# The first output tiles in four rounds of four, the input transposed as it arrives, its squares on ScalarE

## The chip, the cores and the metric

One NeuronCore of one Trainium2 chip runs the whole program in one launch. TensorE (PE) multiplies, VectorE (DVE) and ScalarE (ACT) do the elementwise work and may read PSUM, GpSimd (POOL) does elementwise work in SBUF, and SyncE (SP) issues most of the DMA transfers. The metric is the device time of one execution in microseconds; below 0.2% or so a difference can't be told from none.

## What is computed

The trunk of an encoder: 256 tokens of width 2048 in float32, and two layers. Each layer is a token mixer and a gated MLP with a short convolution, each behind an RMSNorm and added to the residual. Only the start matters here, the first norm and the first projection:

```python
def rms_norm(x, g):
    xf = x.astype(jnp.float32)
    y = xf * lax.rsqrt(jnp.mean(xf * xf, axis=-1, keepdims=True) + EPS)
    return (y * g.astype(jnp.float32)).astype(x.dtype)
...
    for i in range(DEPTH):
        a = rms_norm(h, mix_norm[i])
        ...                               # i = 0: neighbourhood attention
        h = h + mixed
        h = h + conv_glu_ffn(rms_norm(h, ffn_norm[i]), ...)
    return rms_norm(h, final_norm)
```

The first mixer projects `a` to q, k and v (2048 to 3 x 2048), attends within a window with a bias per head, and projects back. The root of the mean square is one number per token. So it can be left out of the projection's input and be multiplied on at its output.

## The kernel before

**Products in two parts.** A float32 matrix is split into a rounded part `hi` and the rest `lo`. `hi` comes from a cast on ScalarE (line 118), `lo` from a subtraction on VectorE (line 119). The activations `a` hold both parts side by side, 256 columns each. A tile of 128 outputs takes, for each 128 inputs (one k, 16 in all), one product of `hi` weights with both parts of `a` (line 156, 512 columns) and one of `lo` weights with the high part (line 159, 256 columns), summed in one of four PSUM tiles `mm`.

**Weights.** `prep_to(n)` brings weights up to chunk n: a DMA on SP's queue into one of five `raw` buffers (line 99), then the cast and the subtraction into one of six `hi` and six `lo` buffers. The main loop at the end of the function goes through `items`, one chunk of one phase each, and calls `prep_to` four chunks ahead (`AHEAD`).

**The order of the work.** The text gives each instruction a place, and work that has to come later is put on a list with `after(n, fn)`, which calls `fn` once n items have been run from where it was called (from the set-up: behind item n). A scheduler of the framework then lays out one queue for each engine: among the instructions that are ready by its reckoning, an engine takes the one that comes first in the text. On the chip each queue is run in that order. A tile with a tag takes one of the buffers of that tag in the order of the text.

**The start.** The first phase projects the q and k of heads 0 to 3, eight output tiles. Its first three tiles (`intro=3`) are interleaved: four rounds over k in steps of four, each round with the three tiles, so that work can start before all of x has come. The other five tiles take chunks of eight k. x comes transposed, in eight loads of 256 KB on SP (line 608), two k each. For each, ScalarE multiplies with the norm's weight and rounds (line 187), and VectorE gives the rest (line 188). GpSimd squares x (line 614) and adds up some of the squares (line 616); in `first_stats` VectorE adds the others (line 622), TensorE sums over the partitions with a matrix of ones (`stats`, line 229), and `rsqrt` takes the root over all 256 tokens, the same in every partition; two small products (line 626) turn it into a column for each half of the tokens.

A finished output tile is scaled by this `rstd` in `normed`: ScalarE copies the right half out of PSUM into a `corr` tile (three buffers), VectorE adds the left half, and then multiplies by `rstd`. Until `first_stats` the finished tiles are held in the text.

The residual `h` holds x by token. It is made by transposing x on TensorE with the identity (`to_tokens`, line 603), copied by VectorE or ScalarE (line 604); this stands behind items 12 to 19. The identity comes with the rest of the parameters, at the end of the set-up (line 618).

**Bias.** Each head's bias is loaded on GpSimd's queue into one of two buffers (line 399) and gets the mask added (line 400); `scores` reads it (line 420).

**Warm-up.** Eight products of a matrix of ones (line 80) run on TensorE before anything has come.

Elsewhere the text has a second way to the root, `token_rstd`, for sums of squares by token: a reduction, `rsqrt` on two columns, and one product with a diagonal matrix (line 259) to spread it over all partitions. The later norms use it.

Of the kernel before, what the change touches and what calls it, by code (L numbers as in the profile page):

```python
# [15 lines left out]
F32 = mybir.dt.float32  # L16
F32R = mybir.dt.float32r
AF = mybir.ActivationFunctionType
# [4 lines left out]
P = 128  # L23
D = 2048
S = 256
KT = D // P
# [8 lines left out]
CH = 8  # L35
AHEAD = 4

S_DOWN = (2, 5, 8)
S_OUT = (1, 3, 5)

# [2 lines left out]
C_SC = C_NORM + 5 * KT  # L43
# [3 lines left out]
C_ID = C_MASK + GRID_W  # L47
# [4 lines left out]
def trunk(ctx, tc, xT, par, bias, wqk, wv, wo, wsc, wscout, wup, wdown, out):  # L52
    nc = tc.nc
    cp = ctx.enter_context(tc.tile_pool(name="const", bufs=1))
    wp = ctx.enter_context(tc.tile_pool(name="wts", bufs=1))
    ap_ = ctx.enter_context(tc.tile_pool(name="acts", bufs=1))
    tp = ctx.enter_context(tc.tile_pool(name="tmp", bufs=2))
    pm = ctx.enter_context(tc.tile_pool(name="pm", bufs=4, space=PSUM))
    pa = ctx.enter_context(tc.tile_pool(name="pa", bufs=1, space=PSUM))

    pt = cp.tile([P, C_END], F32, name="pt")
    h = cp.tile([P, 2, D], F32, name="h")
    ones = cp.tile([P, P], F32, name="ones")
    rstd = cp.tile([P, S], F32, name="rstd")
    acc = cp.tile([P, S], F32, name="acc")
    NPAD = 3
    pads = [cp.tile([P, S + 2], F32, name=f"pad{i}") for i in range(NPAD)]
    pad_at = [0]
# [4 lines left out]

    nc.vector.memset(ones, 1.0)
    nc.scalar.dma_start(out=pt[:, :C_SC], in_=par[:, :C_SC])

    nc.scalar.copy(out=tp.tile([P, 1], F32, name="m", tag="m"), in_=ones[:, :1])
    warm = pa.tile([P, P], F32, name="st", tag="st")
    for _ in range(8):
        nc.tensor.matmul(warm, lhsT=ones, rhs=ones, start=True, stop=True)  # L80
    for p_ in pads:
        nc.gpsimd.memset(p_[:, 0:S + 2:S + 1], 0.0)
    ident = pt[:, C_ID:C_ID + P]
    mask = pt[:, C_MASK:C_MASK + GRID_W]

    def norm_g(n, k):
        return pt[:, C_NORM + n * KT + k:C_NORM + n * KT + k + 1]
# [6 lines left out]
    def prep_to(n):  # L94
        while len(prepped) < min(n, len(chunks)):
            src, w, kind = chunks[len(prepped)]
            raw = wp.tile([P, CH * P], F32, name="raw", tag="raw", bufs=5)
            if kind == "rows":
                nc.sync.dma_start(out=raw[:, :w], in_=src)
                prepped.append(parts(raw[:, :w]) + (raw,))  # L100
                continue

            nc.sync.dma_start(out=raw.rearrange("p (f c) -> p f c", f=4), in_=src.rearrange("f p c -> p f c"))
            r = raw.rearrange("p (f k c) -> p f k c", f=4, c=P)
            if kind == "cols":
                prepped.append(parts(r) + (raw,))
            else:
                prepped.append(sums(prepped[-1][2].rearrange("p (f k c) -> p f k c", f=4, c=P), r))
# [66 lines left out]
    def after(n, fn):  # L175
        later.append((at[0] + n, fn))
# [9 lines left out]
    def scaled_split(dst, src, g):  # L186
        nc.scalar.activation(dst[:, :S], src, AF.Copy, scale=g)
        nc.vector.scalar_tensor_tensor(out=dst[:, S:], in0=src, scalar=g, in1=dst[:, :S].bitcast(F32),  # L188
                                       op0=ALU.mult, op1=ALU.subtract)

    def act_tile():
        return ap_.tile([P, 2 * S], F32R, name="act", tag="act", bufs=HALF)

    def a_tile():
        return ap_.tile([P, 2 * S], F32R, name="a", tag="a", bufs=KT)

    def normed(dst, ps):

        corr = tp.tile([P, S], F32, name="corr", tag="corr", bufs=3)
        nc.scalar.copy(out=corr, in_=ps[:, S:])  # L200
        nc.vector.tensor_add(out=corr, in0=ps[:, :S], in1=corr)  # L201
        nc.vector.tensor_mul(out=dst, in0=corr, in1=rstd)  # L202
# [13 lines left out]
    def rsqrt(dst, v, r, t, sums):  # L216

        nc.vector.tensor_scalar(out=v, in0=sums, scalar1=1.0 / D, scalar2=EPS, op0=ALU.mult, op1=ALU.add)
        nc.scalar.activation(r, v, AF.Sqrt)
        nc.vector.reciprocal(out=r, in_=r)  # L220
        nc.vector.tensor_mul(out=t, in0=r, in1=r)
        nc.vector.scalar_tensor_tensor(out=t, in0=t, scalar=-0.5, in1=v, op0=ALU.mult, op1=ALU.mult)
        nc.vector.scalar_tensor_tensor(out=dst, in0=t, scalar=1.5, in1=r, op0=ALU.add, op1=ALU.mult)

    def stats(sums):

        ps = pa.tile([P, S], F32, name="st", tag="st")
        for i, x in enumerate(sums):
            nc.tensor.matmul(ps, lhsT=ones, rhs=x, start=i == 0, stop=i == len(sums) - 1)
        v = tp.tile([P, S], F32, name="v", tag="v", bufs=1)  # L230
        rt = tp.tile([P, 2, S], F32, name="rt", tag="s")
        rsqrt(rstd, v, rt[:, 0, :], rt[:, 1, :], ps)

    def residual(t, q, ps):
        x = h[:, t, q * 4 * P:(q + 1) * 4 * P]
# [14 lines left out]
    def token_rstd(ssq):  # L250

        v = tp.tile([P, 2], F32, name="z", tag="z")
        nc.vector.tensor_reduce(out=v, in_=ssq, axis=AX.X, op=ALU.add)
        rsqrt(rcol, v, tp.tile([P, 2], F32, name="m", tag="m"), tp.tile([P, 2], F32, name="m", tag="m"), v)
        diag = tp.tile([P, S], F32, name="conv", tag="conv", bufs=4)
        for t in range(2):
            nc.vector.tensor_scalar_mul(diag[:, t * P:(t + 1) * P], ident, rcol[:, t:t + 1])
        bc = pa.tile([P, S], F32, name="st", tag="st")
        nc.tensor.matmul(bc, lhsT=ones, rhs=diag, start=True, stop=True)
        return bc  # L260
# [119 lines left out]
    a0 = [None] * KT  # L380
# [5 lines left out]
    rcol = cp.tile([P, 2], F32, name="rcol")  # L386

    def qk_evac(f, ps):
        h, which = divmod(f, 2)
        x = heads[h]  # L390
        t = tp.tile([P, S], F32, name="qk", tag="conv", bufs=4)
        normed(t, ps)
        if which == 0:
            x["qk"] = tp.tile([P, 4 * S], F32R, name="qk", tag="qk")
        x["qk"[which]] = x["qk"][:, which * 2 * S:(which + 1) * 2 * S]
        split(x["qk"[which]], t)
        if which == 0:
            b = tp.tile([P, 6 * GRID_W], F32, name="bias", tag="bias")
            nc.gpsimd.dma_start(out=b, in_=bias[:, h, :])
            nc.gpsimd.tensor_add(out=b.rearrange("p (i c) -> p i c", c=GRID_W),  # L400
                                 in0=b.rearrange("p (i c) -> p i c", c=GRID_W),
                                 in1=mask.unsqueeze(1).broadcast_to([P, 6, GRID_W]))
            x["b"] = b
        else:
            after(2, lambda: scores(h))
# [115 lines left out]
    def up_evac(layer, act, forms):  # L521
        def evac(f, ps):
# [11 lines left out]
            else:  # L534
# [3 lines left out]
                if j % 2 == 0:  # L538
                    glu["even"] = c
                elif j % HALF // 2 in S_DOWN:  # L540
                    forms[j % HALF // 2] = make_forms(glu["even"], c)
# [37 lines left out]
    def mlp(layer, a, evac):  # L579
        for half in range(2):  # L580
# [3 lines left out]
                  intro=0 if half else 3)  # L584
            Tokens([(wdown[layer, half], HALF)], act, evac if half else residual, S_DOWN, forms)

    for g in range(NH // 4):
        Phase(wqk, range(8 * g, 8 * g + 8), KT, a0, qk_evac, intro=0 if g else 3, step=CH // 2)
        Values(g, a0)
    Tokens([(wo, KT)], oT, to_norm(1, a1))  # L590
    mlp(0, a1, to_norm(2, a2))
# [2 lines left out]
    mlp(1, a3, last_evac())  # L594


    sq = []

    def to_tokens(k, x):
        tr = pa.tile([P, 2, S], F32, name="tr", tag="o" if k % 4 else "tr")  # L600
        for t in range(2):
            for i in range(2):
                nc.tensor.transpose(tr[:, t, i * P:(i + 1) * P], x[:, i * S + t * P:i * S + (t + 1) * P], ident)
        (nc.scalar.copy if k % 4 else nc.vector.tensor_copy)(out=h[:, :, k * P:(k + 2) * P], in_=tr)

    for k in range(0, KT, 2):
        x = act_tile().bitcast(F32)
        nc.sync.dma_start(out=x.rearrange("p (k t) -> p k t", k=2), in_=xT[:, k:k + 2, :])
        for i in range(2):
            a0[k + i] = a_tile()  # L610
            scaled_split(a0[k + i], x[:, i * S:(i + 1) * S], norm_g(0, k + i))
        prep_to(1 + k // 2)
        sq.append(act_tile().bitcast(F32))
        nc.gpsimd.tensor_mul(out=sq[-1], in0=x, in1=x)
        if 2 <= k < KT // 2:
            nc.gpsimd.tensor_add(out=sq[0], in0=sq[0], in1=sq[-1])
        after(12 + k // 2, lambda k=k, x=x: to_tokens(k, x))
    nc.sync.dma_start(out=pt[:, C_SC:], in_=par[:, C_SC:])

    def first_stats():  # L620
        for x in sq[5:]:
            nc.vector.tensor_add(out=sq[4], in0=sq[4], in1=x)
        stats([x[:, i:i + S] for x in (sq[0], sq[4]) for i in (0, S)])
        col = pa.tile([P, 2], F32, name="st", tag="st")
        for t in range(2):
            nc.tensor.matmul(col[:, t:t + 1], lhsT=rstd[:, t * P:(t + 1) * P], rhs=ident[:, :1], start=True, stop=True)
        nc.vector.tensor_copy(rcol, col)
        waiting.clear()
        evacuate()

    after(11, first_stats)

    for i, (ph, ft, c, k0, ka, kb) in enumerate(items):
        at[0] = i
# [76 lines left out]
```

## Time and profile before

| | |
|---|---|
| median of 3 runs | 2243.61 us (2243.46 to 2244.1) |
| profiled execution, its own time | 2245.07 us |
| its span | 2243.2 us |
| mean granted TensorE clock | 0.995 |
| HBM, mean | 188 GB/s |

A busy share counts the time in which an engine's instructions run; TensorE's is modelled at the ends of its products. PEld is the loading of weights into TensorE, which overlaps with products. In a row of groups the columns are: line, engine, operation, out<-in, shapes, count | busy us, mean ns of one | idle us before them <- what ended it. In a row of stretches: the stretch and its length, the busy us of PE, PEld, DVE, ACT and POOL with the number of instructions, the granted clock, the share of DMA and its rate. In a row of the chain or the timeline: start, length, what. In a row of waits: who <- for whom: us in total, times, the longest.

### The profile page before, as it was taken

The page shows a single profiled execution, that of the slowest core. Times are in us where ns is not written, and L with a number is a line of the kernel's source. Part 1 is how long each engine was busy: PE and PEld are TensorE (multiplying, and loading weights), DVE is VectorE, ACT ScalarE, POOL GpSimd, SP SyncE. Part 2 cuts the span into 40 slices and gives each one's busy share as a digit, 9 for nine tenths or more (in the row PEclk, how much of TensorE's full clock was granted, in tenths as well). Part 3 has the DMA queues.
Part 4 walks back from the last instruction along what each step waited for, and adds up shares of the span by engine and source line. Part 5 has one row for each costly group of instructions (what it writes and reads, how often), then busy time and mean ns, then how long its engine had stood idle before and what let it go on. Part 6 is the DMA issues. An engine that isn't in the chain of part 4 may idle for free.

```text
span 2243.2 us, 31742 instructions
## 1 busy us (share of the span) xinstructions
PE 2218.2 (99%) x11818; PEld 1910.4 (85%) x11818; DVE 1745.4 (78%) x2546; ACT 1218.7 (54%) x1822; POOL 84.6 (4%) x110
## 2 busy tenths in 40 slices
PE   7999999999999999999999999999999999999997
PEld 6888888888888888888888888888888888888886
DVE  7777665787888778887877777898888778887876
ACT  5555554555554555555554444566555545555553
POOL 3110000000000000000000000000000000000000
PEclk8999999999999999999999999999999999999999
DMA  6556555555556665555665565565555566555563
GB/s 226 184 178 187 180 173 183 185 188 189 188 175 188 218 196 190 188 186 178 186 212 189 183 195 179 170 224 186 189 189 187 172 203 213 189 189 189 163 193 125
DMA packets 209690, 420.97 MB, mean 188 GB/s; under 512 B 13313, under 2 KB 136193, under 8 KB 209537
## 3 DMA queue, kind: packets, MB, share of 16 engines
q1 hardware_dynamic: 207792, 414.72, 58.3%
q0 software_dynamic: 1024, 3.15, 0.5%
q8 instruction: 93, 1.52, 0.3%
q10 hardware_dynamic: 720, 1.09, 0.1%
q14 instruction: 61, 0.49, 0.1%
HBM read 416.81 MB, written 2.10 MB: 187 GB/s over the span
## 4 chain that ended last, share of the span: by engine, by line
PE 98%; DVE 1%; DMA 0%; ACT 0%; issue 0%; DVEq 0%; SPq 0%
PE mm L156 42%; PE mm L159 22%; PE mm L306 8%; PE mm L308 8%; PE mm L307 8%; PE mm L476 1%; PE mm L478 1%; PE mm L477 1%; PE mu L307 1%; PE mu L306 1%; PE mu L308 1%; PE tr L247 1%; PE tr L438 0%; DMA act<-in_xT 0%; DVE a L575 0%; PE sc L413 0%
## 5 line engine op out<-in xcount | busy, mean ns | idle before, releaser
L119 DVE TENSOR_TENSOR lo<-raw,hi 128x1024 fp32r<-128x1024 f32 (+1 forms) x820 | 988.6, 1212 | 382.6 <-ACT hi L118 374.7
L118 ACT CAST hi<-raw 128x1024 fp32r<-128x1024 f32 (+1 forms) x820 | 839.5, 1027 | 797.1 <-issue 428.2
L156 PE MATMUL mm<-a,hi 128*128 128x512 f32 x4096 | 1035.1, 394 | 8.3 <-DVE a L188 4.8
L156 PEld LDWEIGHTS mm<-a,hi 128*128 128x128 f32 x4096 | 737.5, 189 | 144.0 <-DVE a L188 8.5
L159 PEld LDWEIGHTS mm<-a,lo 128*128 128x128 f32 x4096 | 562.5, 191 | 40.7
L159 PE MATMUL mm<-a,lo 128*128 128x256 f32 x4096 | 575.3, 283 | 0.0
L306 PE MATMUL mm<-hi,act 128*128 128x512 f32 x780 | 304.6, 390 | 0.0
L308 PE MATMUL mm<-hi,act 128*128 128x512 f32 x780 | 304.0, 390 | 0.0
L307 PE MATMUL mm<-lo,act 128*128 128x512 f32 x780 | 303.5, 389 | 0.0
L212 DVE SCALAR_TENSOR_TENSOR conv<-pad,pt,conv 128x256 f32<-128x256 f32 x384 | 184.6, 482 | 9.3 <-ACT conv L210 2.9
L308 PEld LDWEIGHTS mm<-hi,act 128*128 128x128 f32 x780 | 146.4, 188 | 31.2
L307 PEld LDWEIGHTS mm<-lo,act 128*128 128x128 f32 x780 | 146.5, 188 | 30.4
L306 PEld LDWEIGHTS mm<-hi,act 128*128 128x128 f32 x780 | 146.4, 188 | 30.3
L210 ACT ACTIVATE conv<-pad,pt 128x256 f32<-128x256 f32 x176 | 105.3, 600 | 17.0 <-DVE pad L202 17.0
L201 DVE TENSOR_TENSOR corr<-mm,corr 128x256 f32<-128x256 f32 x256 | 106.5, 417 | 0.6
L200 ACT COPY corr<-mm 128x256 f32<-128x256 f32 x256 | 92.5, 362 | 0.3 <-PE mm L159 0.3
L202 DVE TENSOR_TENSOR pad<-corr,rstd 128x256 f32<-128x256 f32 x176 | 74.9, 427 | 5.7
L119 DVE TENSOR_TENSOR lo<-t,hi 128x1024 fp32r<-128x1024 f32 x30 | 36.7, 1225 | 24.3 <-ACT hi L118 24.3
L353 POOL TENSOR_TENSOR s<-conv 128x128 f32<-128x128 f32 x12 | 5.6, 465 | 1257.1 <-DVE conv L535 746.4
L118 ACT CAST hi<-t 128x1024 fp32r<-128x1024 f32 x30 | 31.5, 1049 | 36.3 <-PE mm L308 33.4
L476 PE MATMUL mm<-hi,a 128*128 128x512 f32 x128 | 50.7, 396 | 0.0
L477 PE MATMUL mm<-lo,a 128*128 128x512 f32 x128 | 49.9, 390 | 0.0
(140 smaller groups left out, 1302.8 us busy)
## 6 DMA issues: line engine op xcount, KB each, us to landing
raw<-in_wup SPq DMA_DIRECT2D x352, 512.0 KB, 3.9
raw<-in_wdown SPq DMA_DIRECT2D x176, 512.0 KB, 4.4
raw<-in_wsc SPq DMA_DIRECT2D x96, 512.0 KB, 4.1
raw<-in_wqk SPq DMA_DIRECT2D x58, 512.0 KB, 3.8
raw<-in_wv SPq DMA_DIRECT2D x32, 512.0 KB, 3.8
raw<-in_wo SPq DMA_DIRECT2D x32, 512.0 KB, 3.5
raw<-in_wscout SPq DMA_DIRECT2D x32, 512.0 KB, 4.2
raw<-in_wqk SPq DMA_DIRECT2D x12, 256.0 KB, 4.2
```

Of the source, the lines that this page charges most:

```text
L118: nc.scalar.copy(out=hv, in_=r)
L119: nc.vector.tensor_sub(out=lv, in0=r, in1=hv.bitcast(F32))
L156: nc.tensor.matmul(ps, lhsT=hi[:, o:o + P], rhs=self.src[k], start=k == 0, stop=False)
L159: nc.tensor.matmul(ps[:, S:], lhsT=lo[:, o:o + P], rhs=self.src[k][:, :S], start=False, stop=k == self.nk - 1)
L200: nc.scalar.copy(out=corr, in_=ps[:, S:])
L201: nc.vector.tensor_add(out=corr, in0=ps[:, :S], in1=corr)
L202: nc.vector.tensor_mul(out=dst, in0=corr, in1=rstd)
L210: nc.scalar.activation(c, x[:, 1:S + 1], AF.Identity, scale=w[1], bias=b)
L212: nc.vector.scalar_tensor_tensor(out=c, in0=x[:, tap:tap + S], scalar=w[tap], in1=c, op0=ALU.mult, op1=ALU.add)
L306: nc.tensor.matmul(ps, lhsT=xh, rhs=wh, start=start, stop=False)
L307: nc.tensor.matmul(ps, lhsT=xh, rhs=wl, start=False, stop=False)
L308: nc.tensor.matmul(ps, lhsT=xl, rhs=wh, start=False, stop=stop)
```

## The change

`INTRO` and `STEP`, both 4, set the interleaved tiles and the k of a round: the first four output tiles go in four rounds of four k. x is loaded a round ahead by `load_x`, put among the items with `after`; its scaling is as before. `to_tokens` for the pairs of a round is called behind the first two items of that round. Behind the transposes, ScalarE squares each half out of PSUM and sums it up by token (`accum_out`), and VectorE copies all eight tiles to `h`. GpSimd's squares, their sums and `stats` are gone; `first_stats` is now `token_rstd` of those sums, behind item 14. The identity is loaded second on ScalarE's queue; mask and other parameters come on SP behind item 6. Biases are loaded on SP instead of GpSimd's queue. Twelve warm-up products instead of eight.

```diff
+INTRO = 4
+STEP = 4
...
-    acc = cp.tile([P, S], F32, name="acc")
...
     nc.scalar.dma_start(out=pt[:, :C_SC], in_=par[:, :C_SC])
+    nc.scalar.dma_start(out=pt[:, C_ID:], in_=par[:, C_ID:])
...
-    for _ in range(8):
+    for _ in range(12):
         nc.tensor.matmul(warm, lhsT=ones, rhs=ones, start=True, stop=True)
...
-    def stats(sums):
...
-            nc.gpsimd.dma_start(out=b, in_=bias[:, h, :])
+            nc.sync.dma_start(out=b, in_=bias[:, h, :])
...
-        Phase(wqk, range(8 * g, 8 * g + 8), KT, a0, qk_evac, intro=0 if g else 3, step=CH // 2)
+        Phase(wqk, range(8 * g, 8 * g + 8), KT, a0, qk_evac, intro=0 if g else INTRO, step=STEP)
...
+    ssq0 = cp.tile([P, 2, KT // 2], F32, name="ssq0")
+    xs = {}
+
+    def load_x(k):
+        xs[k] = act_tile().bitcast(F32)
+        nc.sync.dma_start(out=xs[k].rearrange("p (k t) -> p k t", k=2), in_=xT[:, k:k + 2, :])
+        for i in range(2):
+            a0[k + i] = a_tile()
+            scaled_split(a0[k + i], xs[k][:, i * S:(i + 1) * S], norm_g(0, k + i))
+
+    def to_tokens(k):
         tr = pa.tile([P, 2, S], F32, name="tr", tag="o" if k % 4 else "tr")
         for t in range(2):
             for i in range(2):
-                nc.tensor.transpose(tr[:, t, i * P:(i + 1) * P], x[:, i * S + t * P:i * S + (t + 1) * P], ident)
-        (nc.scalar.copy if k % 4 else nc.vector.tensor_copy)(out=h[:, :, k * P:(k + 2) * P], in_=tr)
...
+                nc.tensor.transpose(tr[:, t, i * P:(i + 1) * P], xs[k][:, i * S + t * P:i * S + (t + 1) * P], ident)
+        for t in range(2):
+            nc.scalar.activation(tp.tile([P, S], F32, name="s", tag="s"), tr[:, t, :], AF.Square,
+                                 accum_out=ssq0[:, t, k // 2:k // 2 + 1])
+        nc.vector.tensor_copy(out=h[:, :, k * P:(k + 2) * P], in_=tr)
 
     def first_stats():
...
+        nc.vector.tensor_copy(rstd, token_rstd(ssq0))
         waiting.clear()
         evacuate()
 
-    after(11, first_stats)
+    for r in range(KT // STEP):
+        for i in range(STEP // 2):
+            k = r * STEP + 2 * i
+            if r:
+                after((r - 1) * INTRO + i, lambda k=k: load_x(k))
+            else:
+                load_x(k)
+                prep_to(1 + i)
+            after(r * INTRO + i, lambda k=k: to_tokens(k))
+    after(INTRO + 2, lambda: nc.sync.dma_start(out=pt[:, C_SC:C_ID], in_=par[:, C_SC:C_ID]))
+    after((KT // STEP - 1) * INTRO + 2, first_stats)
```

More of the change, by code (lines that the diff above doesn't have):

```diff
@@ L223, in rsqrt @@
         nc.vector.scalar_tensor_tensor(out=dst, in0=t, scalar=1.5, in1=r, op0=ALU.add, op1=ALU.mult)
-    def stats(sums):
[L227 to L232, printed above, removed]
     def residual(t, q, ps):
@@ L594, in trunk @@
     mlp(1, a3, last_evac())
-    sq = []
-    def to_tokens(k, x):
+    ssq0 = cp.tile([P, 2, KT // 2], F32, name="ssq0")
[7 more added lines that the diff above has]
+    def to_tokens(k):
         tr = pa.tile([P, 2, S], F32, name="tr", tag="o" if k % 4 else "tr")
@@ L602, in to_tokens @@
             for i in range(2):
[L603 to L617, printed above, removed]
@@ L618, in trunk @@
-    nc.sync.dma_start(out=pt[:, C_SC:], in_=par[:, C_SC:])
-    def first_stats():
[L621 to L627, printed above, removed]
+                nc.tensor.transpose(tr[:, t, i * P:(i + 1) * P], xs[k][:, i * S + t * P:i * S + (t + 1) * P], ident)
```

## The prediction

> **What bounds the kernel now.** I read the busy shares first, then the slices, then the busy time by stretch.
>
> ```profile
> PE 2218.2 (99%) x11818; PEld 1910.4 (85%) x11818; DVE 1745.4 (78%) x2546; ACT 1218.7 (54%) x1822; POOL 84.6 (4%) x110
> ...
> PE   7999999999999999999999999999999999999997
> ```
>
> TensorE is busy all the time but in the first and the last of 40 slices. The change touches only the first. The waits of TensorE after 60 us are one row:
>
> ```profile
> PE tr L438 <- DVE s L428: 1.4, 1, 1.4
> ```
>
> So all that can be won here lies before 70 us, and the question is how much. The stretches:
>
> ```profile
> core 0: us, PE busy (x) PEld busy (x) DVE busy (x) ACT busy (x) POOL busy (x), PEclk, DMA share, GB/s
> ...
> 5.95:33.90 27.95, 19.17 (x82) 13.64 (x82) 19.35 (x26) 12.36 (x24) 12.39 (x10) 0.82 0.72 247
> 33.90:38.70 4.80, 4.79 (x19) 4.00 (x20) 2.84 (x4) 2.73 (x4) 1.28 (x2) 0.64 0.39 151
> 38.70:64.00 25.30, 25.30 (x147) 22.07 (x146) 23.84 (x39) 17.16 (x27) 2.24 (x2) 1.00 0.71 229
> 64.00:70.00 6.00, 4.63 (x29) 3.96 (x28) 6.00 (x12) 4.62 (x12) 2.79 (x3) 1.00 0.35 94
> ```
>
> From 5.95 us (the first real matmul) to 33.9 it is idle for 8.8 us, and the busy time is stretched by a clock of 0.5. How much work was done there is counted from the TensorE groups of that stretch, priced by rows of the chain at full clock:
>
> ```profile
> L156 PE MATMUL mm<-a,hi 128*128 128x512 f32 x30 | 12.3, 510 | 7.6 <-DVE a L188 4.1 <-ACT hi L118 3.4
> L159 PE MATMUL mm<-a,lo 128*128 128x256 f32 x24 | 4.8, 334 | 0.0
> L603 PE MATMUL tr<-pt,act 128*128 128x128 f32 x24 | 3.5, 276 | 2.0 <-DMA act<-in_xT 1.6 <-DVE h L604 0.3
> L229 PE MATMUL st<-act,ones 128*128 128x256 f32 x4 | 1.2, 378 | 0.0
> ```
> ```profile
> 38.71 1.82 PE mm L156 x8
> ...
> 45.77 0.86 PE st L229 x4
> ...
> 48.58 0.95 PE mm L159 x8
> ...
> 55.82 0.34 PE st L626 x4
> ...
> 70.46 0.44 PE tr L603 x4
> ```
>
> A hi product costs 0.23 us, a lo product 0.12, a transpose 0.11, a pass of the sums 0.215. The 27.95 us hold 30 x 0.23 + 24 x 0.12 + 24 x 0.11 + 4 x 0.215 = 13.3 us of work, so 14.6 are lost. From 33.9 to 38.7 the clock is 0.64, so 0.36 of 4.8, 1.7 us, are lost. From 64 to 70 it is idle for 1.4. **The start loses 17.7 us** beside the 5.95 in which little can run.
>
> Why it loses them is in SP's queue:
>
> ```profile
> 0.74 0.39 SPq L608 DMA_DIRECT2D act<-in_xT  x1
> 1.19 1.37 SPq L99 DMA_DIRECT2D raw<-in_wqk  x3
> 2.60 0.43 SPq L608 DMA_DIRECT2D act<-in_xT  x1
> 3.08 8.69 SPq L99 DMA_DIRECT2D raw<-in_wqk  x5
> 11.81 0.43 SPq L618 DMA_DIRECT2D pt<-in_par  x1
> 12.29 0.42 SPq L608 DMA_DIRECT2D act<-in_xT  x1
> ...
> 27.68 0.43 SPq L608 DMA_DIRECT2D act<-in_xT  x1
> ```
> ```profile
> SPq L99 <- DVE lo L119: 43.2, 19, 7.9
> ```
>
> The third x load goes out at 12.3 us and the sixth at 27.7, behind weight loads that wait for one of five raw buffers, which VectorE's `lo` subtraction frees. And VectorE is itself slowed:
>
> ```profile
> L188 DVE SCALAR_TENSOR_TENSOR a<-act,pt,a 128x256 fp32r<-128x256 f32 x16 | 12.4, 811 | 5.4 <-ACT a L187 5.4
> L614 POOL TENSOR_TENSOR act<-act 128x512 f32<-128x512 f32 x8 | 9.5, 1192 | 17.5 <-DMA act<-in_xT 17.5
> L119 DVE TENSOR_TENSOR lo<-raw,hi 128x512 fp32r<-128x512 f32 x12 | 9.4, 800 | 4.8 <-ACT hi L118 4.2 <-PE mm L159 0.6
> L187 ACT ACTIVATE a<-act,pt 128x256 fp32r<-128x256 f32 x16 | 7.3, 501 | 6.3 <-DMA act<-in_xT 4.5 <-DMA pt<-in_par 1.8
> L118 ACT CAST hi<-raw 128x512 fp32r<-128x512 f32 x12 | 7.2, 613 | 8.0 <-PE mm L156 5.2 <-DMA raw<-in_wqk 2.7
> L604 DVE COPY h<-tr 128x512 f32<-128x512 f32 x4 | 2.7, 684 | 2.4 <-PE tr L603 2.4
> L220 DVE RECIPROCAL rt<-rt 128x256 f32<-128x256 f32 x1 | 1.8, 1752 | 0.1
> L425 ACT ACTIVATE s<-s,m 128x256 f32<-128x256 f32 x4 | 2.0, 502 | 0.5 <-DVE m L423 0.5
> L425 ACT ACTIVATION_READ_ACCUMULATOR s<-s,m 128x1 f32 x4 | 0.7, 186 | 0.0
> ```
> ```profile
> 42.09 0.87 DVE L188 SCALAR_TENSOR_TENSOR a<-act,pt,a 128x256 fp32r<-128x256 f32 x2
> ```
>
> The same L188 takes 0.435 us when GpSimd is quiet and 0.81 on the mean, with GpSimd's squares (L614) around it: 16 x 0.375 = 6 us of VectorE that the squares cost.
>
> **The change, part by part.** *Squares, sums and the reciprocal root.* Out go GpSimd's squares and adds, three adds on VectorE, eight passes of the sums on TensorE (8 x 0.215 = 1.7 us) and the four small ones to the token column (0.34); in comes one 128x256 fp32 product of two passes (0.43). TensorE: **1.6 us less work**. VectorE's root now runs on two columns where one step alone took 1.75 us over 256. It has cover on TensorE: three correction tiles free three of the four PSUM tiles without the root, so three output tiles of 16 hi and 16 lo (5.6 us each) can run meanwhile. I cost it at nothing; without this cover the root's chain would stand open.
>
> *ScalarE and VectorE instead.* By the Exp row a square with its accumulator read is 0.5 to 0.69 us; I take 0.55, since the read overlaps the next. A round has four. ScalarE per round: four hi casts 2.4, four scalings 2.0, squares 2.2: 6.6 us. VectorE per round: four lo 2.8 (0.7 each: the row's 0.8 holds GpSimd's disturbance, and a copy of that size takes 0.68), four L188 1.7, two copies of h 1.4: 5.9 us. TensorE per round: four items of four hi and four lo at 1.4, eight transposes 0.9: 6.5 us. Three engines are within some tenth of one another. Four rounds of TensorE's work are 26 us.
>
> *The x loads.* They no longer share their buffers' turn with the squares. In the order of the text, the load of round r+1 stands behind at most one weight load that has to wait; hoisted by the scheduler, it stands behind none. Either way it is issued some five items (7 us) ahead of its use. Four output tiles instead of three raise the work per x by a third, so that less of it waits for x.
>
> *The start.* The second x load stands behind one weight load instead of three (256 KB each), and two biases (128 x 384 x 4 bytes each) no longer come in between; 64 KB of identity do. Before, it landed when this began:
>
> ```profile
> 9.82 1.04 POOL L614 TENSOR_TENSOR act<-act 128x512 f32<-128x512 f32 x1 [4.42 <-DMA act<-in_xT]
> ```
> ```profile
> 6.00:8.00 2.00, 0.69 (x2) 0.32 (x2) 0.68 (x2) 0.07 (x1) 0.00 (x0) 0.85 0.98 326
> ```
>
> 832 KB less ahead of it at 326 GB/s are 2.6 us: at 7.2. With scaling and rounding (0.5 and 0.44), k = 2 and 3 are ready from 8.1 on. From the end of the warm-up to there TensorE has half an item or one. I take **2 us lost**, between 0.5 and 4 (x1 lands where it did).
>
> *Twelve warm-up products.*
>
> ```profile
> L80 PE MATMUL st<-ones 128*128 128x128 f32 x16 | 3.4, 401 | 1.1 <-DVE ones L74 1.1
> ...
> 8.00:14.00 6.00, 3.57 (x7) 1.94 (x8) 4.80 (x6) 3.61 (x7) 2.63 (x2) 0.50 0.68 213
> 14.00:17.20 3.20, 3.20 (x13) 2.91 (x12) 2.16 (x4) 1.68 (x4) 1.02 (x2) 0.50 1.00 376
> ```
>
> Eight took 3.4 us from 1.06 on; twelve end at 6.2, just when the first weights are ready, so they delay nothing by more than 0.3. Before, the clock fell to 0.5 after the sparse stretch behind the warm-up and came back after 3.2 us of unbroken work. Whether it falls now is open: not at all (0) or for some 8 us, half of which is lost (4). I take **2**. *The Trainium skill ("TensorE: Matmul & The Clock Gate", "Part 1: The HAM clock gate") has the clock halved after an idle window of about 3.4 us and restored after a busy one. The trace agrees on the second (3.2 us); on the first it looks stricter, since from 8 to 14 the clock is down with TensorE busy 3.57 of 6 us. By the page's idle rule a stretch with small gaps would keep the clock, and the sum would be 2 us lower.*
>
> *Flow through the rounds.* No row shows it. From below: the stretch 38.7 to 64, with VectorE 94% busy and TensorE unbroken, gives 0. From above: TensorE as in 5.95 to 33.9, busy 69% of the time, gives 26/0.69 - 26 = 12 us. It is nearer the first, as x is there and GpSimd is quiet, but three equally loaded engines in one ring with little slack do wait: **5**.
>
> *Bias on SP.* A bias load waits on SP for the scores two heads back, and weight loads queue behind it. But what it waits for and what the weight loads wait for are instructions of VectorE's one ordered queue, so SP waits for nothing longer than it would have; 16 issues of about 0.4 us lie in SP's waits. Nothing; the weights buffered ahead would have to be used up first. *Identity first, the rest of the parameters later*: small, and ahead of their users. Nothing.
>
> *What comes after.* Four heads' halves instead of three now wait for the root, so VectorE has a pile to clear, as in the 1.4 us lost after 64; but its adds and the long root are gone. **1**, between 0 and 3.
>
> **The sum.** Lost after: 2 + 2 + 5 + 1 = 10 instead of 17.7, and 1.6 us less work: 9.3 less. The profiled execution took 2245.07: 2235.8. The median of the runs is 1.46 below it, so against that: **2234.3**. The ends of the terms reach from 0.5 lost (19 us gained) to 23 (4 us worse).
>
> **The rivals.** *Nearly all is won*: TensorE runs unbroken from 8 us on as in 38.7 to 64, 3 us lost: 2245.07 - 14.7 - 1.6 - 1.46 = 2227. For it, the loads; against it, ScalarE loaded as heavily as TensorE.
>
> *The x loads are still late*, since the order on SP is the scheduler's and the weights still wait for raw buffers. Then only the 1.6 us of work go, and perhaps 2 of the 6 us of VectorE's disturbance, the rest lying under the wait for x: 2240. For it, that SP waited 43 us for `lo`; against it, that those loads need no raw buffer.
>
> *The squares tie the engines in a ring* (the slower side). A square waits for its transposes, these stand on TensorE behind products, these wait for a hi cast that stands on ScalarE behind the square. One turn is hi 0.61, lo 0.7, an item at half clock 2.6, transposes 0.5: 4.4 us. All eight tiles at this price lose 35 us, with the 1 us after it 36 against 19.3: 17 worse, 2260. It decides beyond +0.2% from 5.4 tiles in full (24 us). For it, that each engine takes its queue in order; against it, that before the change the copies of h had the same turn and waited 2.4 us on VectorE for four.
>
> **How the numbers follow.** What can be told from no change here is about 0.2%, 4.5 us. Forecast 0.62 (its own range 2230 to 2239), nearly all won 0.12, x still late 0.17, ring 0.09. Faster by more than 0.2% (below 2239.1): the forecast and the first rival, and a little of the second: 0.75. Within: 0.18. Slower: 0.07. The range leaves out the ring and the better half of the first rival: 2228 to 2243.
>
> **What would show it.** Right: all x loads issued before 20 us; L188 near 0.44 us; TensorE's hi products at 0.23 us before 17 us; the first 8k chunk (8 hi in a row) some 10 us earlier. Wrong: ScalarE's casts waiting for TensorE with a square ahead of them (the ring); SP waiting for `lo` ahead of an x load; weights of round 1 landing late because eight x loads went first; TensorE idle at the root's product (L259), or after it for VectorE.

## The result, and the profile after

The changed kernel takes 2229.76 us (median of four, 2229.0 to 2230.07) against 2243.86 (2243.46 to 2244.57): ratio 0.9936, 95% interval 0.9924 to 0.9947, 14.1 us faster. The forecast was 9.3 faster, 2234.3; the time lies inside the range, but 0.2 us below the 2230 to 2239 that the forecast called its own, and nearer the first rival's 2227 than the forecast.

The page's slices of TensorE of the changed kernel:

```profile
PE   9999999999999999999999999999999999999997
```

The first slice is now as full as the rest. Its stretches, with the same bounds as before the change (length, busy us of PE, PEld, DVE, ACT, POOL, granted clock, DMA share, GB/s):

```profile
5.95:33.90 27.95, 27.53 (x163) 23.56 (x162) 23.89 (x40) 23.38 (x67) 2.13 (x2) 1.00 0.93 321
33.90:38.70 4.80, 3.31 (x18) 2.94 (x19) 3.73 (x12) 4.77 (x8) 1.20 (x1) 1.00 0.78 302
38.70:64.00 25.30, 24.41 (x145) 21.11 (x144) 25.12 (x55) 17.08 (x37) 4.09 (x3) 1.00 0.63 200
64.00:70.00 6.00, 6.00 (x33) 5.09 (x32) 4.16 (x8) 2.95 (x5) 2.25 (x1) 1.00 0.77 266
```

In the first stretch TensorE is busy 27.53 us instead of 19.17, at a clock of 1.00 instead of 0.82. What it did there, from the end of the warm-up at 6.2 to 34 us:

```profile
L159 PE MATMUL mm<-a,hi 128*128 128x512 f32 x64 | 19.5, 418 | 0.4 <-DVE a L191 0.3
L162 PE MATMUL mm<-a,lo 128*128 128x256 f32 x64 | 10.2, 282 | 0.0
L605 PE MATMUL tr<-pt,act 128*128 128x128 f32 x32 | 5.1, 272 | 0.0
```

With the prices of the prediction, 64 x 0.23 + 64 x 0.12 + 32 x 0.11 = 25.9 us of work in 27.8: 1.9 lost, where 14.6 were. The x loads in SP's queue:

```profile
1.64 0.42 SPq L596 DMA_DIRECT2D act<-in_xT  x1
...
4.52 0.43 SPq L596 DMA_DIRECT2D act<-in_xT  x1
...
17.74 0.42 SPq L596 DMA_DIRECT2D act<-in_xT  x1
```

The second x goes out at 1.6 (2.6 before), the third at 4.5 (12.3), the last at 17.7 (before, the sixth of eight went out at 27.7). VectorE's two groups of the start, and all that TensorE waits for between 5 and 75 us:

```profile
L122 DVE TENSOR_TENSOR lo<-raw,hi 128x512 fp32r<-128x512 f32 x16 | 10.7, 688 | 2.5 <-ACT hi L121 2.5
L191 DVE SCALAR_TENSOR_TENSOR a<-act,pt,a 128x256 fp32r<-128x256 f32 x16 | 7.1, 478 | 4.1 <-ACT a L190 4.1
```
```profile
PE mm L159 <- DVE z L221: 1.5, 1, 1.5
PE st L253 <- DVE conv L251: 0.7, 1, 0.7
PE mm L159 <- DVE a L191: 0.3, 1, 0.3
PE tr L432 <- DVE act L187: 0.2, 1, 0.2
```

0.69 and 0.48 us for one, instead of 0.80 and 0.81. The one wait of size, 1.5 us, is at 34 to 35.4, when the fifth output tile needs a PSUM tile. Its row names z, a small step of the root that ended last before it; what frees the tile is VectorE's add of the first correction, which ends at 35.25 and stands in VectorE's queue behind a subtraction and the last copy of h:

```profile
34.16 0.68 DVE L609 COPY h<-tr 128x512 f32<-128x512 f32 x1
...
34.84 0.41 DVE L204 TENSOR_TENSOR corr<-mm,corr 128x256 f32<-128x256 f32 x1
```

That nothing came or went later shows in the timeline at the first product with the v weights, a fixed place in the work, before the change and after it:

```profile
77.91 0.40 PE L476 MATMUL mm<-hi,a 128*128 128x512 f32 x1
```
```profile
62.62 0.40 PE L470 MATMUL mm<-hi,a 128*128 128x512 f32 x1
```

It is 15.3 us earlier, and the span is 15.2 us shorter (2228.0 against 2243.2; the profiled execution before lay 1.2 us above its median). All of the gain is made before 63 us.

### The profile page after: what moved, and what is told of

The parts are those of the page before. It is cut to its first block, busy times and chain, and to the rows that moved or that the text cites. A ratio compares the mean times of both kernels' runs of the same rounds, so it can differ in the third digit from the quotient of the medians.

```text
span 2228.0 us, 31792 instructions
## 1 busy us (share of the span) xinstructions
PE 2211.2 (99%) x11816; PEld 1908.1 (86%) x11816; DVE 1735.9 (78%) x2552; ACT 1221.2 (55%) x1852; POOL 63.1 (3%) x83
## 4 chain that ended last, share of the span: by engine, by line
PE 97%; DVE 1%; ACT 1%; DMA 0%; issue 0%; SPq 0%; DVEq 0%; ACTq 0%
PE mm L159 41%; PE mm L162 21%; PE mm L300 8%; PE mm L302 8%; PE mm L301 8%; PE mm L470 1%; PE mm L472 1%; PE mm L471 1%; PE mu L301 1%; PE mu L300 1%; PE mu L302 1%; PE tr L241 1%; DVE lo L122 0%; PE tr L432 0%; DMA raw<-in_wqk 0%
## 5 line engine op out<-in xcount | busy, mean ns | idle before, releaser
L470 PE MATMUL mm<-hi,a 128*128 128x512 f32 x128 | 50.7, 396 | 0.0
L472 PE MATMUL mm<-hi,a 128*128 128x512 f32 x128 | 49.9, 390 | 0.0
```

## The experiments

The theory taken into them: late x loads are the main loss, and GpSimd's disturbance of VectorE the second, half hidden. The rivals: the disturbance; the four tiles; the clock. Times are compared with the kernel before, or with the changed kernel (2229.76, and 2229.66 in a later run).

**1. The x loads freed, in the kernel before.** The squares go into buffers that nothing uses yet, so that x tiles and squares no longer take turns.

```diff
-        sq.append(act_tile().bitcast(F32))
+        sq.append(sq_tile())          # halves of tiles of the tags vv, sf and qk
```

> The kernel before, with one thing changed: GpSimd's squares lie in buffers of their own instead of taking turns with the x tiles, so that the x loads stand on SP between the weight loads one by one. Squares, sums, three interleaved tiles and eight warm-up products stay. Theory (late x loads are the main loss): 6 to 10 us faster than before, 2234 to 2238, with L188 still near 0.8 us. Rival (the disturbance of VectorE by GpSimd is the main loss): less than 3 us faster. Rival (four rounds of four tiles are what counts): less than 3 us faster.

2240.58 against 2244.16: ratio 0.9987 (0.9978 to 0.9996), 3.6 us. On SP the x loads now stand one by one between the weight loads, so the edit did what it was for, but it brought only some half of the least that was expected, and a little more than the rivals allowed. Its first stretch, its L188 and TensorE's three longest waits:

```profile
5.95:33.90 27.95, 21.39 (x92) 15.56 (x92) 24.70 (x30) 12.46 (x26) 15.35 (x12) 0.88 0.65 216
```
```profile
L188 DVE SCALAR_TENSOR_TENSOR a<-act,pt,a 128x256 fp32r<-128x256 f32 x16 | 13.8, 898 | 4.8 <-ACT a L187 4.8
```
```profile
PE mm L159 <- DVE lo L119: 4.1, 4, 1.2
PE mm L156 <- DVE a L188: 3.1, 4, 1.3
PE st L634 <- DVE rstd L223: 2.3, 1, 2.3
```

With x there, VectorE is busy 24.70 of 27.95 us, L188 is slower still (0.90), and TensorE waits for VectorE's `lo` instead of for x. One cause hid behind the other. The third wait is new too: the sums over the partitions end at 36.9 us instead of 46.6, and now TensorE waits 2.3 us for the root before the small products that turn it into columns.

**2. The x loads tied, in the changed kernel.**

```diff
             scaled_split(a0[k + i], xs[k][:, i * S:(i + 1) * S], norm_g(0, k + i))
+        tie = act_tile().bitcast(F32)
+        nc.gpsimd.tensor_copy(out=tie[:, :1], in_=xs[k][:, :1])
```

> The changed kernel, with a tile between any two x tiles that GpSimd writes (one column) once x is there, so that the x loads take turns as before the change; no squares on GpSimd. Theory (late x loads): 2 to 6 us slower than the changed kernel, 2232 to 2236. Rivals (GpSimd's disturbance, or the number of tiles): within 1 us of the changed kernel, 2229 to 2231.

2233.38 (2232.88 to 2235.55), 3.6 slower than the changed kernel, as the theory had it. The third x load goes out at 6.8 us and the last at 24.6 (4.5 and 17.7 without the tie; before the change the third at 12.3 and the last two from 29.8 on), so the tie is weaker than the one before the change. TensorE now waits for x's parts and for x itself:

```profile
PE mm L159 <- DVE a L191: 2.9, 4, 1.2
PE tr L607 <- DMA act<-in_xT: 1.5, 2, 0.9
```

Its L191 takes 554 ns in the mean instead of 478, but the small copies are not the reason. Seven of its eight pairs take 0.87 or 0.88 us, as in the changed kernel; the last, late with its x, falls beside GpSimd's adds of the mask to the bias and takes 2.06:

```profile
32.57 2.14 POOL L394 TENSOR_TENSOR bias<-bias,pt 128x384 f32<-128x384 f32 x2
32.93 2.06 DVE L191 SCALAR_TENSOR_TENSOR a<-act,pt,a 128x256 fp32r<-128x256 f32 x2
```

**3. The squares back on GpSimd, in the changed kernel.**

```diff
+        sq.append(ap_.tile([P, 2 * S], F32, name="sq", tag="sq", bufs=1))
+        nc.gpsimd.tensor_mul(out=sq[-1], in0=xs[k], in1=xs[k])
+        if 2 <= k < KT // 2:
+            nc.gpsimd.tensor_add(out=sq[-1], in0=sq[-1], in1=xs[k])
```

> The changed kernel, with GpSimd squaring each x tile and adding three more times, results unused, in a buffer of its own: the disturbance alone. L188 should be near 0.8 us again. Theory (the prediction's 6 us of VectorE, half of it hidden): 2 to 4 us slower than the changed kernel, 2232 to 2234. Rival (hidden under TensorE's work wholly): within 0.7 us, 2229 to 2230.5.

2236.67 (2232.89 to 2237.45), 6.9 slower (five of its six executions lie above 2236): more than the theory's 2 to 4, so next to nothing is hidden.

```profile
L122 DVE TENSOR_TENSOR lo<-raw,hi 128x512 fp32r<-128x512 f32 x16 | 14.1, 912 | 1.2 <-ACT hi L121 1.2
L191 DVE SCALAR_TENSOR_TENSOR a<-act,pt,a 128x256 fp32r<-128x256 f32 x16 | 10.9, 716 | 3.9 <-ACT a L190 3.9
```

Against the changed kernel the two groups take 16 x (0.912 - 0.688) + 16 x (0.716 - 0.478) = 7.4 us more: VectorE's loss and the kernel's are about the same.

**4. Eight warm-up products, in the changed kernel.**

```diff
-    for _ in range(12):
+    for _ in range(8):
```

> The changed kernel with eight warm-up products instead of twelve. If the four more hold the clock: it falls to 0.5 for some 5 to 8 us and 2 to 4 us are lost, 2232 to 2234. If the early x holds it: the clock stays at 1.0 and the time within 0.7 us, 2229 to 2230.5.

2230.25 (2229.39 to 2230.65), within 0.5 of the changed kernel: the four more products do nothing that can be told. The clock stays up without them, through a wait of TensorE of 1.3 us for the identity:

```profile
3.00:6.00 3.00, 1.83 (x9) 1.54 (x8) 0.88 (x2) 1.22 (x4) 0.00 (x0) 1.00 0.94 273
...
8.00:14.00 6.00, 5.86 (x32) 4.97 (x33) 5.78 (x12) 6.00 (x18) 0.00 (x0) 1.00 0.91 299
```

**5 and 6. GpSimd quiet, in the kernel before**, with the loads freed as in 1 and with the loads as they were. The buffers are filled with ones instead of squares.

```diff
-        nc.gpsimd.tensor_mul(out=sq[-1], in0=x, in1=x)
-        if 2 <= k < KT // 2:
-            nc.gpsimd.tensor_add(out=sq[0], in0=sq[0], in1=sq[-1])
+        nc.gpsimd.tensor_copy(out=sq[-1][:, :1], in_=x[:, :1])     # in 6 alone: keeps the turns
+        nc.gpsimd.memset(sq[-1], 1.0)
```

> The kernel before with the x loads freed as in the run that freed them alone, and GpSimd's squares and their three sums left out: the buffers are filled with ones, so that the root is of a constant. The adds on VectorE, the sums on TensorE and the three interleaved tiles stay. Theory (the two causes stand behind one another: with x early, VectorE slowed by GpSimd is what TensorE waits for): 9 to 12 us faster than before, 2232 to 2235, more than the 3.6 us of the freed loads and the next run's gain together or about their sum. Rival (four rounds of four tiles carry the rest): not below 2237.

> The kernel before with GpSimd's squares and sums left out (one column copied once x is there, then filled with ones), the x loads still taking turns: the quiet alone. L188 near 0.45 us. Theory (late x hides most of the disturbance): 1 to 4 us faster than before, 2240 to 2243. Rival (the disturbance is the main loss): 6 or more, 2238 or less.

Quiet alone: 2239.10 against 2243.61, ratio 0.9980 (0.9971 to 0.9989), 4.5 us, between what the theory and the rival gave. Both: 2231.65, ratio 0.9944 (0.9927 to 0.9961), **12.0 us**. The two alone give 3.6 + 4.5 = 8.1; together they give 3.9 more. Of both, the first stretch and L188:

```profile
5.95:33.90 27.95, 25.00 (x127) 21.19 (x127) 20.80 (x37) 17.07 (x33) 2.76 (x2) 0.88 0.79 269
```
```profile
L188 DVE SCALAR_TENSOR_TENSOR a<-act,pt,a 128x256 fp32r<-128x256 f32 x16 | 7.1, 483 | 0.8 <-ACT a L187 0.7
```

VectorE falls from the freed kernel's 24.70 us to 20.80, and TensorE's 21.39 rise to 25.00. So run 5 has 12.0 of the 14.1 us, with three tiles, eight warm-up products and the sums still on TensorE. Two things in it are more than the two causes. The squares themselves are left out; the changed kernel has them on ScalarE. And ones need no x: run 5's sums end at 23.3 us, and the root's small products run at 32.9 us without a wait, where run 1 waited 2.3 us. So up to 2.3 of the 3.9 us may come from the earlier root and not from a faster VectorE; these runs do not part the two.

**7 and 10. Three interleaved tiles, in the changed kernel**, twice, the second time beside the changed kernel (run 9) on one chip.

```diff
-INTRO = 4
+INTRO = 3
```

> The changed kernel with three interleaved tiles instead of four (INTRO = 3), all else kept; the fourth PSUM tile is free again. If four tiles are needed to cover the x loads: 2 to 4 us slower than the changed kernel, 2232 to 2234. Rival (x is early enough, and the fourth tile only brings the wait of 1.5 us for a PSUM tile): within 1 us, or up to 1.5 faster, 2228 to 2230.5.

> The changed kernel once more, on the same chip as the next three: 2229 to 2231.

> The changed kernel with three interleaved tiles once more, beside the changed kernel itself. If three are better than four: 1.5 to 3 us faster than the run before this, 2227 to 2228.5. If the 2.3 us were the chip's: within 0.7 us of it.

2227.44 (2226.97 to 2228.12), then 2227.64 (2227.19 to 2227.86) beside 2229.66 (2228.51 to 2230.64). No run with three is as slow as the fastest with four: three tiles are **2.0 us faster** than the change, 0.9925 (0.9913 to 0.9938) of the kernel before, and the fastest version found. In the first of the two no wait of TensorE after 5 us is longer than 0.2; in the second the longest is for the root:

```profile
PE mm L159 <- ACT hi L121: 0.2, 1, 0.2
```
```profile
PE st L253 <- DVE conv L251: 0.6, 1, 0.6
```

With three, the last squares and the root come three items earlier and a PSUM tile is free. ScalarE's first copies out of PSUM, in the changed kernel and with three tiles:

```profile
33.29 0.93 ACT L203 COPY corr<-mm 128x256 f32<-128x256 f32 x3
```
```profile
26.43 0.67 ACT L203 COPY corr<-mm 128x256 f32<-128x256 f32 x2
```

Run 5 has three tiles as well. Beside it 4.2 us remain (2231.65 against 2227.44) for the rest of the change, the 1.6 us of work among them, and for a pause in run 5 that is shown below.

**8. PSUM freed early, in the changed kernel**: the copy and the add of a finished tile stand where it is finished, and get a fourth buffer.

```diff
-                held.append((self, ft))
+                held.append((self, ft, corrected(self.ps.pop(ft))))
...
+    def corrected(ps):
+        corr = tp.tile([P, S], F32, name="corr", tag="corr", bufs=4)
+        nc.scalar.copy(out=corr, in_=ps[:, S:])
+        nc.vector.tensor_add(out=corr, in0=ps[:, :S], in1=corr)
+        return corr
```

> The changed kernel, with the first two steps of a finished tile (ScalarE's copy, VectorE's add) put where the tile is finished instead of behind the root, and a fourth buffer for their result, so that PSUM is free when the fifth tile needs it. Theory (the 1.5 us that TensorE waits at 34 us is PSUM held by these steps): 1 to 1.5 us faster than the changed kernel, 2228 to 2229. Rival (the wait only moves to the root's product or to VectorE): within 0.5 us, 2229.3 to 2230.3.

2230.91 (2229.86 to 2231.86): not faster, and 0.6 us above the rival's range. The wait of 1.5 us is gone, and all that TensorE waits for is now

```profile
PE st L256 <- DVE conv L254: 1.9, 1, 1.9
```

the root's product with the diagonal matrix (line 256 here). The rival was right that the wait only moves: TensorE waits 1.9 us at one place instead of 1.5 and 0.7 at two. With four tiles the root is late, and PSUM freed early does not help.

**11. The biases on GpSimd's queue, in the changed kernel.**

```diff
-            nc.sync.dma_start(out=b, in_=bias[:, h, :])
+            nc.gpsimd.dma_start(out=b, in_=bias[:, h, :])
```

> The changed kernel with the biases loaded on GpSimd's queue as before the change. The prediction's price for SP is nothing. But two biases of 192 KB then come in the first microseconds, beside the x and weight loads: 384 KB at some 320 GB/s are 1.2 us, of which 0 to 1.2 are lost: 2229.5 to 2231. Rival (weights wait behind a bias on SP's queue in the changed kernel, so that GpSimd's queue is better): 1 to 2 us faster.

2231.00 (2230.73 to 2232.25), 1.3 slower than the changed kernel beside it. k = 2 is ready 0.3 us later, as expected; its first product in this run, and in the changed kernel:

```profile
7.89 0.50 PE L159 MATMUL mm<-a,hi 128*128 128x512 f32 x1 [0.95 <-DVE a L191]
```
```profile
7.56 0.50 PE L159 MATMUL mm<-a,hi 128*128 128x512 f32 x1
```

But the wait of TensorE for the softmax that the kernel before had is back too, so how the 1.3 us divide is not settled:

```profile
PE tr L432 <- DVE s L422: 1.4, 1, 1.4
```

**12. The identity with the other parameters, in the changed kernel.**

```diff
-    nc.scalar.dma_start(out=pt[:, C_ID:], in_=par[:, C_ID:])
...
-    after(INTRO + 2, lambda: nc.sync.dma_start(out=pt[:, C_SC:C_ID], in_=par[:, C_SC:C_ID]))
+    nc.sync.dma_start(out=pt[:, C_SC:], in_=par[:, C_SC:])
```

> The changed kernel with the identity in one load with the other parameters (472 KB) on SP behind the first two x and weight loads, as far forward as the order allows. Transposes, squares and copies of the first round come some 1 to 2 us later, and a load of 472 KB goes ahead of weights: 1.5 us. If the identity's place matters: 1 to 3 us slower, 2231 to 2233, with TensorE waiting for the parameters. Rival (the products fill the gap): within 0.7 us.

2231.39 (2230.65 to 2232.55), 1.7 slower. TensorE does not wait for the identity anywhere; what grows is the wait for the PSUM tile, from 1.5 to

```profile
PE mm L158 <- DVE z L220: 2.3, 1, 2.3
```

The expected size was right, the expected place was not. ScalarE is not what holds the tile: its first copy out of PSUM is at 33.14, a little earlier than the changed kernel's 33.29. But VectorE's first add of a correction is at 35.40 instead of 34.84, behind the last copy of h (34.73 instead of 34.16). So it is VectorE's queue that frees the tile late. In run 8, where the add stands where the tile is finished, the wait for PSUM was gone; in this run that was not tried.

## Why the prediction came out as it did

**Where the gain lies: right.** The start lost 17.7 us, the gain could only be a part of that and of 1.6 us of work, and it was all made before 63 us.

**The sum.** Lost after, by the prices and the stretches: 1.9 up to 34 us, then 1.5 and 0.9 idle; 4.3 where 10 were forecast. With the 1.6 us of work and 0.25 for the later end of the warm-up that is 17.7 - 4.3 + 1.6 - 0.25 = 14.8, against 15.2 of the spans. The terms:

- *The start* (2, between 0.5 and 4) and *the flow through the rounds* (5, between 0 and 12) were together 7 and measured 1.9. **This is the mis-sized term**: the flow was priced between two stretches and should have stood at the lower. ScalarE is busy 23.38 and VectorE 23.89 of 27.95 us with TensorE almost unbroken; here two engines loaded to 84 and 85% did not make the third wait, with its inputs prepared four chunks ahead. ScalarE's load was also priced too high: 16 squares at 0.36 us instead of 0.55 are 3 us less.
- *The clock* (2): 0. It is 1.00 in every stretch up to 70 us.
- *What comes after* (1, between 0 and 3): 2.4, and not where I put it. I gave the root's chain no cost since three correction tiles would free three PSUM tiles without it. They did not: VectorE's add, the second half of each correction, stood in its queue behind the last copy of h and freed the first tile only at 35.25 us, 1.3 us after the fifth output tile needed it. Experiment 8 shows that with PSUM free TensorE waits for the root itself, and 7 that four tiles cost 2 us against three. **That step, "I cost it at nothing", failed.**
- *Bias on SP, nothing*: right that it costs nothing. SP does wait for the scores, and no wait of TensorE for weights follows. Experiment 11 gives the move a worth of at most some 1.3 us; the prediction had that gain under the start. SP's waits before 70 us in the changed kernel:

```profile
SPq L102 <- DVE lo L122: 31.6, 25, 3.8
SPq L393 <- DVE s L414: 6.8, 3, 3.9
```

- *Four tiles raise the work per x*: true, and not needed. The sentence put a benefit on the part of the change that costs 2 us.

**The reasons.** Both causes named were real, but their weights were not as the sum took them: the late x and the disturbance of VectorE stand one behind the other on one path. Freeing x alone gives 3.6 us, because VectorE is then what TensorE waits for; quiet alone gives 4.5; both give 12.0, up to 2.3 of it by the earlier root of run 5. The rival "x loads still late" took only 2 us for the quiet, "the rest lying under the wait for x"; the run shows 4.5.

**The rivals.** "Nearly all is won" was the nearest. The ring did not form; all that ScalarE waited for with a square at its head is

```profile
ACT s L607 <- PE tr L605: 0.5, 1, 0.5
```

**The signs.** The last x load was issued at 17.7 us and L191 (the new L188) took 0.48, as the right ones had it. The first chunk of eight k came at 35.39 instead of 38.55, 3 us earlier and not 10; but a fourth tile's four items, 5.6 us of work, now lie ahead of it. Two of the signs of a wrong prediction were there as well. SP waited for `lo` ahead of x loads (7.2 us before 20 us, none longer than 1.2), without harm: TensorE waited 0.3 us for x's parts. And TensorE was idle at the root's product, for 0.7 us.

**The clock.** The twelve warm-up products are not what holds it: with eight, it stays at 1.00 in the changed kernel. In run 5, with eight and x freed, TensorE paused for 2.8 us in the profiled execution, the slowest of its four (2233.97), because weights had not landed, and the clock fell. Its timeline, and two stretches within the pause:

```profile
10.48 1.22 PE L156 MATMUL mm<-a,hi 128*128 128x512 f32 x2 [2.82 <-ACT hi L118]
```
```profile
8.50:9.00 0.50, 0.00 (x0) 0.00 (x0) 0.00 (x0) 0.00 (x0) 0.00 (x0) 1.00 1.13 385
9.25:9.50 0.25, 0.00 (x0) 0.00 (x0) 0.00 (x0) 0.00 (x0) 0.00 (x0) 0.50 0.96 377
```

By the modelled end of its last product TensorE is idle from 7.65 us on, so the clock fell some 1.6 us into the pause, and this execution loses part of its difference to the changed kernel there. In run 1 a pause of 2.3 us, behind 11 us without a gap, left the clock at 1.00:

```profile
44.75:47.07 2.32, 0.00 (x1) 0.00 (x0) 2.32 (x6) 2.15 (x3) 0.00 (x0) 1.00 0.65 191
```

So the length of a pause alone does not decide it; the two differ in what ran before. In run 5 that was three hi products and two passes of the sums in 1.8 us, 1.1 us of work at the prediction's prices. The Trainium skill ("TensorE: Matmul & The Clock Gate", "Part 1: The HAM clock gate") asks for an idle window of about 3.4 us; in run 5 an idle time of 1.6 us behind such work was enough. By its rule the term of the clock would have been 0, and 0 was measured, with no pause longer than 1.5 us.

## What to carry to other kernels

Two causes of a stall on one path have to be taken away together, and an experiment that takes one away shows only how soon the next one begins. Work that an idle engine does to spare a busy one can cost the busy one as much as if it did the work itself: in experiment 3 it cost VectorE 7.4 us, where eight squares and three adds at the 0.69 us of its subtraction would take 7.6 (an estimate). Look at the same instruction's mean with and without the neighbour. And tiles of one tag take turns in the order of the text, so a short-lived tile among prefetched ones ties the prefetch to the work.

## What the runs showed of the hardware

GpSimd slows VectorE when it reads: beside squares and adds, the products of run 3 take 0.72 instead of 0.48 us, and the subtractions 0.91 instead of 0.69. The copies of h out of PSUM are not slower there (0.68 against 0.69). Beside fills the products are not slowed either. In run 6 a pair of them beside a fill takes 0.88 us, and a pair beside an add of the mask to the bias, which reads, takes 1.49:

```profile
9.75 0.88 DVE L188 SCALAR_TENSOR_TENSOR a<-act,pt,a 128x256 fp32r<-128x256 f32 x2
9.94 0.53 POOL L615 MEMSET act<- 128x512 f32 x1
...
17.54 1.00 POOL L400 TENSOR_TENSOR bias<-bias,pt 128x384 f32<-128x384 f32 x1
17.73 1.49 DVE L188 SCALAR_TENSOR_TENSOR a<-act,pt,a 128x256 fp32r<-128x256 f32 x2
```

The Trainium skill ("SBUF — State Buffer", "Who interferes with whom") says that a VectorE instruction with two SBUF inputs contends with a GpSimd instruction that reads SBUF, not with one that only writes it; these runs agree. A square on ScalarE is cheaper than the 0.55 us that was taken: the reading of its accumulator starts within it, and the next square within the reading, 0.36 us from start to start. From the changed kernel's timeline:

```profile
30.91 0.37 ACT L607 ACTIVATE s<-tr 128x256 f32<-128x256 f32 x1
31.18 0.19 ACT L607 ACTIVATION_READ_ACCUMULATOR s<-tr 128x1 f32 x1
31.27 0.38 ACT L607 ACTIVATE s<-tr 128x256 f32<-128x256 f32 x1
```
